# Diff heads' p, their rows and all of y turned by VectorE and transfers instead of TensorE, in a fused decoder layer

## The chip, the cores and the metric

The kernel runs on one core of a Trainium2 chip. Its engines each execute their own instruction stream in order: TensorE (PE, with PEld for the weight loads that overlap the matmuls), VectorE (DVE), ScalarE (ACT), GpSimd (POOL) and SyncE (SP). Here GpSimd issues transfers (its software queue) and SyncE issues the weight loads. The metric is the device time of one execution in microseconds (us).

## The reference

One decoder layer over 256 tokens of width 2048, in float32: a half-step SwiGLU feed-forward (5632 wide), layer norm, a token mixer with two attention branches, a projection and layer norm, a second feed-forward and a last layer norm. The branch that the change touches is differential attention, four heads of two score maps each:

```python
s = jnp.einsum('bqhmd,bkhmd->bhmqk', q[:, q0:q1], k[:, :q1]).astype(jnp.float32) * scale
...
p = jax.nn.softmax(s, axis=-1)
a = (p[:, :, 0] - lam * p[:, :, 1]).astype(v.dtype)
outs.append(jnp.einsum('bhqk,bkhd->bqhd', a, v[:, :q1]))
...
o_diff = (_rms_norm(o_diff, subln_g) * (1.0 - lambda_init)).reshape(b, s, DIFF_V_COLS)

y = jax.nn.sigmoid(gate_mla) * (o_mla @ w_br_mla) + jax.nn.sigmoid(gate_diff) * (o_diff @ w_br_diff)
return y @ w_out
```

The other branch is multi-head latent attention (MLA, eight heads), whose queries, keys and values come out of low-rank rows by `w_uq`, `w_uk` and `w_uv`. Queries are taken in blocks of 128, and the first block sees only the first 128 keys, so a head's probabilities are three 128x128 squares: a tile of 128x384.

## The kernel before

**Products.** Every large product is made of float32 parts rounded to the matmul's type: a value is split in a high part (a cast on ScalarE, line 154) and a low part (a subtraction on VectorE, line 155), and three matmuls (high by high, high by low, low by high: lines 208, 209, 210) make one product of a 128x128 stationary tile with 512 weight columns. Weights arrive raw by SP's queue and are split into a ring of six slots (`wring`). A unit of the program is the twelve matmuls of one weight tile of 128x1024 (two 128-row halves, two blocks of 128 tokens, three products each).

**Order.** The program is written in one stream. `unit()` and `advance()` keep a few units loaded and split ahead of the products, each unit ends with a `tick()`, and `later(n, fn)` puts work off by n ticks: transposes, softmax steps and copies are woven between the units by such numbers. A scheduler then fixes the order on each engine and places the semaphores; `issue_after` and `behind_split` tie one instruction behind another. Tiles called `blocks`, `turned`, `qr`, `junk`, `orow` and the like come from one pool of six slots (`tmp`), so a new one waits until the last reader of an old one, which may be a transfer, has ended.

**Stages.** First feed-forward (0 to 685 us): its hidden rows are turned by `turn_out` (VectorE transposes 32x32 blocks, line 715, and four GpSimd transfers write them to DRAM so that the rest of the turn is made by addresses, line 717), to be read back as `hraw` (line 893) and split as `h`. Layer norm and the mixer (685 to 1180), the output projection with a layer norm (1180 to 1320), and the second feed-forward (1320 to 1971), built as the first.

**The mixer's narrow part** (about 985 to 1180 us) runs `gate(1, 2)`, `wuq` (three column chunks), `wuk` (two), `wuv` (two), `gate(1, 3)`, `wbd` (four) and `wbm` (four). The four differential heads are woven between `gate(1, 2)` and `wuv`: `scores` (line 1228, then softmax), `turn` (three transposes of p by TensorE, line 1103, and a copy out of PSUM, line 1105), `values` (lines 1248 to 1250, then root mean square and `orow`, line 1261), and `turn2` (four transposes of `orow` by TensorE, line 1268, split straight into `od`, the left operand of `wbd`). They start six ticks apart. The MLA heads follow in the same manner and keep their transposes. `cols_proj` copies a projection's bank by ScalarE to a row tile (line 1160), turns it by `turn_out`, and reads it back by `turned` (line 729) for `qT` and `kT`; the rotary part `qr` goes the same way. In the output projection's left operand y, quads 0 and 1 are turned by transfers and quads 2 and 3 by TensorE (`rows_to_quad`, line 671).

Of the kernel before, what the change touches and what calls it, by code (L numbers as in the profile page):

```python
# [59 lines left out]
def layer_kernel(ctx: ExitStack, tc: tile.TileContext, a: dict, out: bass.AP):  # L60
# [89 lines left out]

    cast, lows, fetched = [None], [None], [None]

# [559 lines left out]
    def turn_out(row, to):  # L712

        t = tmp_tile([P, 512], "blocks")
        V.transpose(t, row)  # L715
        for i in range(4):
            nc.gpsimd.dma_start(to.rearrange("(g r) (i f) -> i r g f", g=4, i=4)[i],  # L717
                                t[32 * i:32 * (i + 1), :].rearrange("r (g f) -> r g f", g=4))
# [3 lines left out]

    def turn(row, use, wait, more):
        to = dram.tile([P, 512], F32, name=nm("turn"))
        turn_out(row, to)

        def back():
            t = tmp_tile([P, 512], "turned")
            nc.gpsimd.dma_start(t, to)
            later(more, lambda: use(turned(t)))  # L730
        later(wait, back)

    def turn_to_quad(row, b, x, q, wait, more):
        turn(row, lambda t: x.put(q, b, t), wait, more)

# [116 lines left out]
    def ffn(n, x, wgu, wdn, residual, g, bt, each, first=None, between=None, nxt=None, cols=None, norm=None, pending=None):  # L852
# [7 lines left out]
        def half(c, b, up, gate, wait=0):  # L860
# [7 lines left out]
            def product():  # L868
                V.tensor_tensor(out=hb[b, q][:, o:o + 256], in0=up, in1=sg, op=ALU.mult)
            if wait:  # L870
# [19 lines left out]
        def get_h(q):  # L890
            raw = got[q] = act_tile([P, 2, 512], F32, "hraw")
            for b in range(2):
                nc.gpsimd.dma_start(raw[:, b, :], hT[q, b])

# [205 lines left out]
    def p_cols(p):  # L1100
# [5 lines left out]
        return pt  # L1106

    def mixer(x):
        c_row = [act_tile([P, 1024], F32, "c_row") for _ in range(2)]
# [44 lines left out]

        def cols_proj(w, xx, kt, name, k0=0, more=10):
# [29 lines left out]
        def pair_cols(w, name):  # L1185
            dst = [act_tile([P, 4, T], F32, name) for _ in range(2)]

            def done(n, b, bank, snap, op):
                t = tmp_tile([P, 512], name + "r")
                whole(t, bank, snap, op)  # L1190
                later(1, lambda: turn_to_cols(t, dst[n], b, 4, 10))
            hy.group(w[0], w[1], done, False, True)
# [12 lines left out]
        def c_back(j):  # L1205
            if j == 0:
                for key, src in turns.items():
                    back[key] = tmp_tile([P, 512], "turned")
                    nc.gpsimd.dma_start(back[key], src)
# [6 lines left out]

        od = Acts(MH, "od")

        def diff_head(h):
# [21 lines left out]
            def turn():  # L1241
                st["pt"] = p_cols(st["p"])

            def values():
# [13 lines left out]
                r = rstd(ms, RMS_EPS, 2)  # L1258
                orow = tmp_tile([P, 512], "orow")
                for b in range(2):  # L1260
                    V.scalar_tensor_tensor(out=orow[:, b * DV:(b + 1) * DV], in0=o[:, b * DV:(b + 1) * DV],
                                           scalar=r[:, b:b + 1], in1=subg, op0=ALU.mult, op1=ALU.mult)
                st["o"] = orow

            def turn2():
                t = tr_bank()
                for i in range(4):
                    PE.transpose(t[:, i * P:(i + 1) * P], st["o"][:, i * P:(i + 1) * P], ident)
                tv = t.rearrange("p (b i t) -> p b i t", b=2, i=2)
                for b in range(2):  # L1270
                    od.put(h // 2, b, tv[:, b], (h % 2) * 2, 2)
            return scores, turn, values, turn2
# [8 lines left out]
        def qr_done(b, bank):  # L1281
            t = tmp_tile([P, 512], "qr")
            tv = t.rearrange("p (j h i) -> p j h i", j=2, h=MH)
            rope(tv[:, 0], tv[:, 1], bank, b, MH)
            later(1, lambda: turn_to_cols(t, qrT, b, 4, 10))
        project(a["wuq"][2], cn, 4, 512, qr_done)
        kT = [cols_proj(a["wuk"][c], cn, 4, "kT", 4, 8) for c in range(2)]
        v = [act_tile([P, 1024], F32, "v") for _ in range(2)]
# [56 lines left out]
        def branch_mla(f):  # L1345
# [87 lines left out]
def _layout(i):  # L1433
# [27 lines left out]
    r["wbm"] = _chunks(w["w_branch_mla"], 512)  # L1461
    r["wbd"] = _chunks(w["w_branch_diff"], 512)
    r["w_out"] = _chunks(np.concatenate([_turned_rows(w["w_out"][:1024]), w["w_out"][1024:]]), 512)
    pos = i["positions"]
# [32 lines left out]
```

## Time and profile before

| | |
|---|---|
| median of 3 runs | 1973.18 us (1972.44 to 1976.2) |
| the profiled execution | 1972.85 us, span 1971.1 us |
| TensorE busy | 1955.1 us (99% of the span), mean granted clock 0.998 |
| VectorE, ScalarE, GpSimd busy | 1773.5 us (90%), 1265.5 us (64%), 291.0 us (15%) |
| GpSimd's turn writes (`turn<-blocks`) | 104 of 64 KB, 3.4 us from issue to landing |

All times below are in us from the start of the span. A group's row gives the engine, the operation, the tiles out<-in, the count, then busy time and mean ns of one, then the idle time of the engine just before. A row of waits gives who waited for whom: us in total, times, and the longest. A row of the timeline gives start, duration, engine, line and operation. Matmuls overlap their successors, so the time from one start to the next is what a matmul takes of TensorE, not its own duration.

### The profile page before, as it was taken

Reading aid. Unit: us, or ns where it says so; the run is one execution under the profiler, and the core shown is the slowest. Engines: PE = TensorE matmul, PEld = TensorE weight load, DVE = VectorE, ACT = ScalarE, POOL = GpSimd, SP = SyncE. Lnnn points to the kernel's source line nnn. Section 1 sums busy time; section 2 is a strip of 40 time slices with the busy share of each in tenths; the row PEclk is TensorE's granted clock in tenths of the full one; section 3 lists DMA queues with packets and bytes.
Section 4 is the critical chain, followed back from the end, with each engine's and each line's share of the span. In section 5 each row is a group of like instructions: output and inputs, shape, how many; then the busy total and the mean of one; then the engine's idle time right before and its main releaser. Section 6 shows DMA issues by size and latency. Waiting matters only on the chain.

```text
span 1971.1 us, 25747 instructions
## 1 busy us (share of the span) xinstructions
PE 1955.1 (99%) x8784; PEld 1620.0 (82%) x8784; DVE 1773.5 (90%) x2175; ACT 1265.5 (64%) x1650; POOL 291.0 (15%) x503
## 2 busy tenths in 40 slices
PE   9999999999999999999999999999999999999997
PEld 7888888888888898888888888888888888888886
DVE  7999999999998879988976677789999999999986
ACT  6666767676655566666667765556676776665661
POOL 0112111122100010102223120001211112210000
PEclk9999999999999999999999999999999999999999
DMA  8978888777776666767667668578888878786763
GB/s 309 287 227 262 285 270 251 235 216 281 296 235 222 209 218 254 244 224 259 223 198 241 234 216 271 199 263 254 254 263 294 243 243 249 238 321 237 274 234 124
DMA packets 147478, 485.71 MB, mean 246 GB/s; under 512 B 20961, under 2 KB 21009, under 8 KB 147345
## 3 DMA queue, kind: packets, MB, share of 16 engines
q1 hardware_dynamic: 117360, 397.99, 58.2%
q0 software_dynamic: 29984, 86.07, 16.4%
q8 instruction: 69, 1.13, 0.2%
q14 instruction: 65, 0.52, 0.1%
HBM read 455.13 MB, written 28.84 MB: 246 GB/s over the span
## 4 chain that ended last, share of the span: by engine, by line
PE 95%; DVE 2%; DMA 1%; issue 1%; ACT 0%; SPq 0%; DVEq 0%; ACTq 0%
PE mm L209 30%; PE mm L210 30%; PE mm L208 30%; DVE wring L155 1%; PE tr L208 1%; PE tr L210 1%; PE tr L209 1%; DMA sraw<-in_gu_dram 1%; PE tr L671 0%; DVE sraw L428 0%; ACT wring L154 0%; DMA raw<-in_gu_dram 0%; PE tr L1228 0%; PE tr L1301 0%; PE tr L1303 0%
## 5 line engine op out<-in xcount | busy, mean ns | idle before, releaser
L154 ACT CAST wring<-raw 128x1024 fp32r<-128x1024 f32 (+2 forms) x467 | 482.2, 1038 | 296.5 <-PE mm L210 207.2
L155 DVE TENSOR_TENSOR wring<-raw,wring 128x1024 fp32r<-128x1024 f32 (+2 forms) x467 | 559.1, 1206 | 95.4 <-ACT wring L154 92.8
L154 ACT CAST wring<-sraw 128x1024 fp32r<-128x1024 f32 x436 | 454.8, 1054 | 230.2 <-DVE sraw L428 94.2
L155 DVE TENSOR_TENSOR wring<-sraw,wring 128x1024 fp32r<-128x1024 f32 x436 | 523.2, 1228 | 21.6 <-ACT wring L154 18.8
L210 PE MATMUL mm<-wring,h 128*128 128x512 f32 (+2 forms) x1248 | 480.2, 385 | 0.0
L208 PE MATMUL mm<-wring,h 128*128 128x512 f32 (+2 forms) x1248 | 480.2, 385 | 0.0
L209 PE MATMUL mm<-wring,h 128*128 128x512 f32 (+2 forms) x1248 | 479.8, 385 | 0.0
L209 PE MATMUL mm<-wring,xs 128*128 128x512 f32 x776 | 302.2, 389 | 1.3 <-DVE wring L155 1.3
L208 PE MATMUL mm<-wring,xs 128*128 128x512 f32 x776 | 302.2, 389 | 0.0
L210 PE MATMUL mm<-wring,xs 128*128 128x512 f32 x776 | 302.0, 389 | 0.0
L209 PEld LDWEIGHTS mm<-wring,h 128*128 128x128 f32 x1248 | 234.5, 188 | 46.8 <-DVE wring L155 0.7
L210 PEld LDWEIGHTS mm<-wring,h 128*128 128x128 f32 x1248 | 234.5, 188 | 46.5 <-DVE h L155 0.7
L208 PEld LDWEIGHTS mm<-wring,h 128*128 128x128 f32 x1248 | 234.4, 188 | 46.4 <-ACT h L154 0.6
L428 DVE TENSOR_TENSOR sraw<-sraw,sraw 128x1024 f32<-128x1024 f32 x168 | 200.2, 1229 | 3.5 <-DMA sraw<-in_wdv_dram 1.6
L209 PEld LDWEIGHTS mm<-wring,xs 128*128 128x128 f32 x776 | 145.7, 188 | 32.5 <-DVE wring L155 2.3
L208 PEld LDWEIGHTS mm<-wring,xs 128*128 128x128 f32 x776 | 145.7, 188 | 30.1
L210 PEld LDWEIGHTS mm<-wring,xs 128*128 128x128 f32 x776 | 145.7, 188 | 30.0
L717 POOL DMA_DIRECT2D hT<-blocks x176 | 97.1, 562 | 370.0 <-DVE blocks L715 368.2
L208 PE MATMUL mm<-wring,x 128*128 128x512 f32 x336 | 130.8, 390 | 0.8 <-ACT wring L154 0.8
L209 PE MATMUL mm<-wring,x 128*128 128x512 f32 x336 | 131.0, 390 | 0.5 <-DVE wring L155 0.5
L210 PE MATMUL mm<-wring,x 128*128 128x512 f32 x336 | 130.6, 389 | 0.0
L430 POOL DMA_DIRECT2D sraw<-in_gu_dram x40 | 35.6, 900 | 359.4 <-DVE sraw L428 309.0
(307 smaller groups left out, 2289.6 us busy)
## 6 DMA issues: line engine op xcount, KB each, us to landing
sraw<-in_gu_dram SPq DMA_DIRECT2D x160, 512.0 KB, 5.4
raw<-in_gu_dram SPq DMA_DIRECT2D x159, 512.0 KB, 4.7
raw<-in_dn_dram SPq DMA_DIRECT2D x140, 512.0 KB, 4.7
sraw<-in_gu_dram POOLq DMA_DIRECT2D x40, 512.0 KB, 6.9
sraw<-in_dn_dram SPq DMA_DIRECT2D x36, 512.0 KB, 5.6
hraw<-hT POOLq DMA_DIRECT2D x68, 256.0 KB, 6.2
eraw<-in_gu_dram SPq DMA_DIRECT2D x64, 256.0 KB, 6.0
raw<-in_w_out_dram SPq DMA_DIRECT2D x32, 512.0 KB, 4.3
```

Of the source, the lines that this page charges most:

```text
L154: cast[0] = S.copy(hi, src)
L155: lows[0] = V.tensor_tensor(out=lo, in0=src, in1=hi.bitcast(F32), op=ALU.subtract)
L208: PE.matmul(o, xh, wh, start=first, stop=False, skip_group_check=again)
L209: PE.matmul(o, xh, wl, start=False, stop=False, skip_group_check=again)
L210: PE.matmul(o, xl, wh, start=False, stop=last, skip_group_check=again)
L428: last = V.tensor_tensor(out=R[src][i], in0=R[src][i], in1=R[add[1]][i], op=ALU.add)
L430: nc.gpsimd.dma_start(R["12"][s], source("22", s), accum_op=ALU.add)
L717: nc.gpsimd.dma_start(to.rearrange("(g r) (i f) -> i r g f", g=4, i=4)[i], t[32 * i:32 * (i + 1), :].rearrange("r (g f) -> r g f", g=4))
```

## The change

It has five parts.

1. **p of the differential heads.** `p_cols` (three TensorE transposes, one ScalarE copy) gives way to `turn_p`: VectorE transposes p's 32x32 blocks into `pblocks` (128x384), one GpSimd transfer writes it to DRAM (`pturn`), and two ticks later four GpSimd transfers of 32 partitions each read it back in runs of 32 numbers (`pt<-pturn`).
2. **The heads' rows.** `turn2` goes. Two heads share an `orow` tile (from the larger pool of activation tiles), and after the second of a pair `turn_to_quad` turns both blocks: two VectorE transposes, eight transfers out, two back, and whole splits in place of half ones. `w_branch_diff` and `w_out` get their rows permuted on the host to match.
3. **All of y** goes through `turn_to_quad`, quads 2 and 3 with shorter waits.
4. **The projections' rows.** `cols_proj` hands the PSUM bank itself to the VectorE transpose (eight ScalarE copies go), with `more` 5 in place of 10 or 8; quads turned back get a tile of the larger pool (`roomy`).
5. **Places.** Heads start 5 ticks apart with steps at 0, 3 and 8; in the feed-forwards `get_h` is tied behind the last hidden write before it (`turned_out`), and the delayed `product` is tied behind a split.

```diff
+        with tc.issue_after(turned_out[0].ins):
+            for b in range(2):
+                nc.gpsimd.dma_start(raw[:, b, :], hT[q, b])
...
+    def turn_p(p, keep, more):
+        t = tmp_tile([P, 384], "pblocks")
+        V.transpose(t, p)
+        to = dram.tile([P, 384], F32, name=nm("pturn"))
+        nc.gpsimd.dma_start(to, t)
+        def back():
+            pt = small.tile([P, 384], F32, tag="p", name=nm("pt"), bufs=3)
+            for k in range(4):
+                nc.gpsimd.dma_start(pt[32 * k:32 * (k + 1), :].rearrange("f (b i c) -> f b i c", b=3, i=4),
+                                    to.rearrange("(i f) (b k c) -> k f b i c", i=4, b=3, k=4)[k])
+            keep["pt"] = pt
+        later(more, back)
...
             def done(b, bank):
-                t = tmp_tile([P, 512], name + "r")
-                S.copy(t, bank)
-                later(1, lambda: turn_to_cols(t, dst, b, 4, more))
+                later(1, lambda: turn_to_cols(bank, dst, b, 4, more))
...
             def turn():
-                st["pt"] = p_cols(st["p"])
+                turn_p(st["p"], st, 2)
...
-            def turn2():
-                t = tr_bank()
-                for i in range(4):
-                    PE.transpose(t[:, i * P:(i + 1) * P], st["o"][:, i * P:(i + 1) * P], ident)
-                tv = t.rearrange("p (b i t) -> p b i t", b=2, i=2)
-                for b in range(2):
-                    od.put(h // 2, b, tv[:, b], (h % 2) * 2, 2)
+                if h % 2 == 1:
+                    rows = orows.pop(h // 2)
+                    for b in range(2):
+                        later(2 + b, lambda b=b: turn_to_quad(rows[:, b, :], b, od, h // 2, 2, 3))
...
-                later(2 + 6 * h + 3 * i + i // 3, f)
+                later(1 + 5 * h + (0, 3, 8)[i], f)
...
-                if f < 2:
-                    later(1, lambda: turn_to_quad(y[:, b, :], b, yq, f, 4, 6))
-                else:
-                    later(2, lambda: rows_to_quad(y[:, b, :], b, yq, f))
+                later(1, lambda: turn_to_quad(y[:, b, :], b, yq, f, *((4, 6) if f < 2 else (3, 3) if f == 2 else (1, 2))))
```

**Head 2.** In the rows below the numbers behind a name tell tiles apart; heads are counted from 0. On GpSimd, before, the turns of `qr` and the first `kT` rows stand alone between one another:

```order
L717 DMA turn_8221<-blocks_8222 32x4x128 x4
L729 DMA turned_8253<-turn_8057 128x512
L717 DMA turn_8255<-blocks_8256 32x4x128 x4
L729 DMA turned_8281<-turn_8096 128x512
L717 DMA turn_8283<-blocks_8284 32x4x128 x4
L729 DMA turned_8316<-turn_8123 128x512
```

In the change the write of head 2's p (`pturn_8203`) and its reading back (`pt_8312`) have the two `qr` turns and the turn of the first pair's row (`turn_8305`, out of `blocks_8306`) between them:

```order
L1115 DMA pturn_8203<-pblocks_8201 128x384
L729 DMA turned_8205<-turn_8027 128x512
L717 DMA turn_8207<-blocks_8208 32x4x128 x4
L729 DMA turned_8239<-turn_8095 128x512
L717 DMA turn_8241<-blocks_8242 32x4x128 x4
L729 DMA turned_8303<-turn_8119 128x512
L717 DMA turn_8305<-blocks_8306 32x4x128 x4
L1120 DMA pt_8312<-pturn_8203 32x12x32 x4
L717 DMA turn_8317<-blocks_8318 32x4x128 x4
```

On VectorE, before, head 1's row (`orow_8178`) is followed by the softmax of the next head's scores and by two weight splits:

```order
L1261 SCALAR_TENSOR_TENSOR orow_8178<-tr_8154,f_8176,subg 128x256 x2
L1084 SCALAR_TENSOR_TENSOR st_8184<-tr_8181,bias_93 128x384
L1084 SCALAR_TENSOR_TENSOR st_8200<-tr_8197,bias_93 128x384
L1086 TENSOR_REDUCE mx_8186<-st_8184 128x1
L1087 TENSOR_REDUCE mx_8186<-st_8184 128x1
L715 STREAM_TRANSPOSE blocks_8222<-qr_8140 128x512
L1089 TENSOR_SCALAR nmx_8189<-mx_8186 128x2
L155 TENSOR_TENSOR wring_103<-raw_8392,wring_102 128x1024
L1071 TENSOR_TENSOR ropec_8247<-mm_8147,sincos 128x512
L155 TENSOR_TENSOR wring_5086<-raw_8477,wring_5085 128x1024
```

In the change the row of head 1 (`orow_8003`, shared with head 0) is followed by head 3's softmax, two weight splits, and then the transpose that `turn_8305` writes out:

```order
L1280 SCALAR_TENSOR_TENSOR orow_8003<-tr_8175,f_8197,subg 128x256 x2
L1086 SCALAR_TENSOR_TENSOR st_8268<-tr_8265,bias_94 128x384
L1086 SCALAR_TENSOR_TENSOR st_8284<-tr_8281,bias_94 128x384
L1088 TENSOR_REDUCE mx_8270<-st_8268 128x1
L1089 TENSOR_REDUCE mx_8270<-st_8268 128x1
L155 TENSOR_TENSOR wring_117<-raw_8524,wring_116 128x1024
L1091 TENSOR_SCALAR nmx_8273<-mx_8270 128x2
L155 TENSOR_TENSOR wring_115<-raw_8545,wring_114 128x1024
L715 STREAM_TRANSPOSE blocks_8306<-orow_8003 128x512
```

So GpSimd's reading of head 2's p now stands behind a transpose of head 1's finished row. On TensorE, the transposes of head 2's p and head 1's row before:

```order
L210 MATMUL mm_8337<-wring_114,cn_7861 128x512
L1103 MATMUL tr_8310<-ident,p_8191 128x128
L1268 MATMUL tr_8344<-ident,orow_8178 128x128 x2
L1103 MATMUL tr_8310<-ident,p_8191 128x128 x2
L1268 MATMUL tr_8344<-ident,orow_8178 128x128 x2
L208 MATMUL mm_8368<-wring_102,cn_7834 128x512
```

and around the values of head 2 in the change, which take `pt_8312`:

```order
L209 MATMUL mm_8459<-wring_103,cn_7856 128x512
L210 MATMUL mm_8459<-wring_102,cn_7857 128x512
L1265 MATMUL tr_8405<-dv_7343,pt_8312 128x256
L1266 MATMUL tr_8405<-dv_7343,pt_8312 128x256
L1267 MATMUL tr_8405<-dv_7344,pt_8312 128x256
L208 MATMUL mm_8473<-wring_5085,cn_7836 128x512
L209 MATMUL mm_8473<-wring_5086,cn_7836 128x512
```

What moved is the release of the values: from a ScalarE copy behind TensorE's own transposes to the last of four transfers on GpSimd's queue. From the values of head 0 to those of heads 1, 2 and 3 there are 79, 47 and 69 matmuls of 512 columns in the change (and head 3's scores just behind head 1's values).

**Head 3.** On VectorE, before, between the last `kT` transposes and head 2's `oms` (the first step of its root mean square) stand four weight splits:

```order
L715 STREAM_TRANSPOSE blocks_8356<-kTr_8335 128x512
L155 TENSOR_TENSOR wring_103<-raw_8587,wring_102 128x1024
L155 TENSOR_TENSOR wring_5086<-raw_8631,wring_5085 128x1024
L155 TENSOR_TENSOR wring_119<-raw_8648,wring_118 128x1024
L715 STREAM_TRANSPOSE blocks_8386<-kTr_8381 128x512
L155 TENSOR_TENSOR wring_117<-raw_8666,wring_116 128x1024
L1257 TENSOR_SCALAR oms_8418<-oss_8414 128x2
L690 TENSOR_SCALAR ve_8420<-oms_8418 128x2
```

In the change three transposes, each into a `blocks` tile of the pool of six, stand ahead of two splits, `oms` and the transpose of head 3's p:

```order
L715 STREAM_TRANSPOSE blocks_8345<-orow_8003 128x512
L715 STREAM_TRANSPOSE blocks_8352<-mm_8258 128x512
L715 STREAM_TRANSPOSE blocks_8380<-mm_8329 128x512
L155 TENSOR_TENSOR wring_5086<-raw_8630,wring_5085 128x1024
L155 TENSOR_TENSOR wring_119<-raw_8654,wring_118 128x1024
L1274 TENSOR_SCALAR oms_8413<-oss_8409 128x2
L1113 STREAM_TRANSPOSE pblocks_8432<-p_8275 128x384
```

and on GpSimd the write of head 3's p and the four reads come after the writes of those transposes, the reads divided by the turn of another `kT` row:

```order
L717 DMA turn_8351<-blocks_8352 32x4x128 x4
L729 DMA turned_8375<-turn_8207 128x512
L729 DMA turned_8377<-turn_8305 128x512
L717 DMA turn_8379<-blocks_8380 32x4x128 x4
L1115 DMA pturn_8434<-pblocks_8432 128x384
L729 DMA turned_8439<-turn_8344 128x512
L729 DMA turned_8437<-turn_8241 128x512
L1120 DMA pt_8494<-pturn_8434 32x12x32
L717 DMA turn_8441<-blocks_8442 32x4x128 x4
L729 DMA turned_8467<-turn_8317 128x512
L729 DMA turned_8488<-turn_8351 128x512
L1120 DMA pt_8494<-pturn_8434 32x12x32 x3
```

What moved here is that head 2's row of work and head 3's p on VectorE stand behind three turns, and that eight transfers of other tiles stand between the write of head 3's p and the last of its reads.

**The hidden rows.** In the first feed-forward four of GpSimd's rows stood behind an early hidden write, ahead of the weight loads of the next group:

```order
 L717 DMA hT_122<-blocks_1833 32x4x128 x4
 L717 DMA hT_122<-blocks_1839 32x4x128 x4
-L893 DMA hraw_3231<-hT_122 128x512
-L893 DMA hraw_3282<-hT_122 128x512 x2
-L893 DMA hraw_3231<-hT_122 128x512
```

In the change the first three quads (two transfers each) stand together behind the last but one group's hidden write:

```order
 L717 DMA hT_122<-blocks_3061 32x4x128 x4
 L717 DMA hT_122<-blocks_3067 32x4x128 x4
+L895 DMA hraw_3201<-hT_122 128x512 x2
+L895 DMA hraw_3231<-hT_122 128x512 x2
+L895 DMA hraw_3282<-hT_122 128x512 x2
 L430 DMA sraw_462<-in_gu_dram 128x1024
 L430 DMA sraw_463<-in_gu_dram 128x1024
```

The second feed-forward has the same shift. ScalarE's casts of the first of these quads go with them.

More of the change, by code (lines that the diff above doesn't have):

```diff
@@ L721, in turned, with turn @@
         return v.rearrange("p (i k c) -> p k i c", i=4, k=4)
-    def turn(row, use, wait, more):
+    def turn(row, use, wait, more, roomy=False):
         to = dram.tile([P, 512], F32, name=nm("turn"))
@@ L727, in back @@
         def back():
-            t = tmp_tile([P, 512], "turned")
+            t = act_tile([P, 512], F32, "turned") if roomy else tmp_tile([P, 512], "turned")
             nc.gpsimd.dma_start(t, to)
@@ L733, in turn_to_quad @@
     def turn_to_quad(row, b, x, q, wait, more):
-        turn(row, lambda t: x.put(q, b, t), wait, more)
+        turn(row, lambda t: x.put(q, b, t), wait, more, True)
     def turn_to_cols(row, dst, b, wait, more):
@@ L868, in product @@
             def product():
-                V.tensor_tensor(out=hb[b, q][:, o:o + 256], in0=up, in1=sg, op=ALU.mult)
+                with behind_split(3) if wait else nullcontext():
+                    V.tensor_tensor(out=hb[b, q][:, o:o + 256], in0=up, in1=sg, op=ALU.mult)
             if wait:
@@ L1206, in c_back @@
             if j == 0:
-                for key, src in turns.items():
-                    back[key] = tmp_tile([P, 512], "turned")
-                    nc.gpsimd.dma_start(back[key], src)
+                pairs = [act_tile([P, 2, 512], F32, "turned") for _ in range(2)]
+                for (i, b), src in turns.items():
+                    back[i, b] = pairs[i][:, b, :]
+                    nc.gpsimd.dma_start(back[i, b], src)
             if j >= 4:
```

28 lines of the change are left out of this document (14 added, 14 removed).

## The prediction

> **What bounds the kernel now.** First the page: the share of each engine, the granted clock, and the chain that ended last.
>
> ```profile
> span 1971.1 us, 25747 instructions
> PE 1955.1 (99%) x8784; PEld 1620.0 (82%) x8784; DVE 1773.5 (90%) x2175; ACT 1265.5 (64%) x1650; POOL 291.0 (15%) x503
> PEclk9999999999999999999999999999999999999999
> PE 95%; DVE 2%; DMA 1%; issue 1%; ACT 0%; SPq 0%; DVEq 0%; ACTq 0%
> ```
>
> TensorE is the bound: 16.0 us of the span are not busy, and 95% of the chain is its own. What it saves counts in full, and every wait of it counts too. Then the busy time by stretch: the narrow part of the mixer, and the two places where the early hidden rows are read back.
>
> ```profile
> 1006.00:1082.00 76.00, 74.69 (x346) 61.70 (x345) 56.08 (x123) 55.67 (x105) 28.43 (x52) 1.00 0.72 236
> 232.00:260.00 28.00, 27.27 (x121) 22.28 (x120) 26.06 (x32) 18.58 (x25) 7.85 (x13) 1.00 0.94 309
> 1498.00:1535.00 37.00, 36.47 (x161) 29.80 (x160) 35.38 (x42) 24.67 (x34) 9.22 (x15) 1.00 0.85 273
> ```
>
> In 1006 to 1082, where the differential heads lie, TensorE idles 1.3 us of 76, VectorE is 74% busy, and GpSimd issues 52 transfers. So the heads cost TensorE almost only their instructions. Last the timeline of TensorE, for what an instruction takes of it (start to start).
>
> ```profile
> 1025.71 0.39 PE L208 MATMUL mm<-wring,cn 128*128 128x512 f32 x1
> 1026.39 0.60 PE L1248 MATMUL tr<-dv,pt 128*128 128x256 f32 x2
> 1027.69 1.47 PE L1228 MATMUL tr<-dkT,dqT 128*128 128x128 f32 x8
> 1028.81 0.58 PE L208 MATMUL mm<-wring,cn 128*128 128x512 f32 x1
> 1042.61 0.27 PE L1103 MATMUL tr<-ident,p 128*128 128x128 f32 x1
> 1043.15 0.38 PE L1268 MATMUL tr<-ident,orow 128*128 128x128 f32 x2
> ```
>
> A triple takes 1026.39 - 1025.71 = 0.68, so a matmul of 512 columns 0.227; a head's values 1.30, its scores 1.12. Five transposes start between 1042.61 and 1043.15: 0.108 each.
>
> **What goes.** The groups and waits of the removed work:
>
> ```profile
> L1103 PE MATMUL tr<-ident,p 128*128 128x128 f32 x36 | 7.3, 284 | 0.2 <-DVE p L1237 0.2
> L1268 PE MATMUL tr<-ident,orow 128*128 128x128 f32 x16 | 3.1, 274 | 0.0
> L671 PE MATMUL tr<-ident,diff 128*128 128x128 f32 x16 | 2.4, 272 | 0.0
> L1248 PE MATMUL tr<-dv,pt 128*128 128x256 f32 x8 | 2.5, 392 | 1.1 <-ACT pt L1105 1.1
> ```
>
> Of the 36 transposes of p, 24 belong to the eight MLA heads and stay; 12 go, with 16 of `orow` and 16 of y. 44 x 0.108 = 4.8 us of TensorE. The wait of 1.1 for `pt` and the 0.2 for p go with them: 1.3. ScalarE's copies and half splits lie beside TensorE's matmuls (64% busy): nothing.
>
> The early reading of hidden rows, in the timeline of GpSimd:
>
> ```profile
> 237.20 2.17 POOL L893 DMA_DIRECT2D hraw<-hT  x4 [2.13 <-DMA hT<-blocks]
> 253.52 0.89 POOL L430 DMA_DIRECT2D sraw<-in_gu_dram  x1 [14.14 <-DVE sraw L428]
> 293.38 0.91 POOL L430 DMA_DIRECT2D sraw<-in_gu_dram  x1 [16.32 <-DVE sraw L428]
> ```
>
> The four reads end at 239.4, 14 us ahead of GpSimd's next weight load, so they don't hold the queue; what is lost at 232 to 260 (0.73 by the stretch) and at 1498 to 1535 (0.53) comes with their traffic or ScalarE's casts. The change puts six such reads behind a later hidden write, where no edge weights follow. The loss goes (1.3 gained), or moves along and grows by half (0.6 lost, 6 reads for 4). I take 0.8: the new place has less weight traffic. Gains: 4.8 + 1.3 + 0.8 = 6.9 us.
>
> **What comes.** Rows of the new work and of what it waits for:
>
> ```profile
> L717 POOL DMA_DIRECT2D turn<-blocks x104 | 56.8, 554 | 168.3 <-DVE blocks L715 139.8 <-DVE ms L1126 18.4 <-DVE nmx L1089 6.7
> turn<-blocks POOLq DMA_DIRECT2D x104, 64.0 KB, 3.4
> turned<-turn POOLq DMA_DIRECT2D x26, 256.0 KB, 4.3
> cols<-in_ln_cols_dram POOLq DMA_DIRECT2D x2, 16.0 KB, 3.5
> L715 DVE STREAM_TRANSPOSE blocks<-kTr 128x512 f32<-128x512 f32 x4 | 2.8, 707 | 5.2 <-DMA turn<-blocks 5.1
> DVE blocks L715 <- DMA turn<-blocks: 5.1, 1, 5.1
> ACT wring L154 <- PE mm L210: 269.9, 267, 5.9
> ```
>
> A turn write of four transfers is 2.2 us of GpSimd and lands 3.4 later; a transpose is 0.7 of VectorE; and a transpose has already stood 5.1 us for a turn write, the tile of the pool of six that it needed still being read. The four reads of p have no row: 384 runs of 128 bytes each. I take 0.55 for the issue, as every turn transfer, and 3.5 for the landing, that of `cols` (128 runs of 128 bytes). Three times the runs at three times the price (1.65) is the upper end; they can't be cheaper, being transfers from the same queue.
>
> *Head 2.* Count from the end of head 1's values. Before, that end is 1027.69, and the row follows so:
>
> ```profile
> 1027.89 0.39 ACT L1254 ACTIVATE junk<-tr 128x256 f32<-128x256 f32 x1 [0.25 <-PE tr L1250]
> 1029.74 0.17 DVE L1257 TENSOR_SCALAR oms<-oss 128x2 f32<-128x2 f32 x1
> 1031.18 0.88 DVE L1261 SCALAR_TENSOR_TENSOR orow<-tr,f,subg 128x256 f32<-128x256 f32 x2
> 1031.97 1.01 DVE L1084 SCALAR_TENSOR_TENSOR st<-tr,bias 128x384 f32<-128x384 f32 x2
> 1033.42 0.70 DVE L715 STREAM_TRANSPOSE blocks<-qr 128x512 f32<-128x512 f32 x1
> 1034.08 1.22 DVE L155 TENSOR_TENSOR wring<-raw,wring 128x1024 fp32r<-128x1024 f32 x1
> 1035.21 0.69 DVE L1071 TENSOR_TENSOR ropec<-mm,sincos 128x512 f32<-128x512 f32 x1
> ```
>
> `orow` is done 4.4 behind the values; st and the two mx take 1.4 (1031.97 to 1033.42). In the change two splits (start to start 1.13 each) and `blocks_8306` (0.7) follow: 4.4 + 1.4 + 2.3 + 0.7 = 8.8. Then `turn_8305` 2.2, the four reads 2.2, landing 3.5: 16.7. TensorE meanwhile has head 3's scores and 47 matmuls: 1.12 + 47 x 0.227 = 11.8. It waits 4.9 at least. In the change the rotary rows (transpose, ropec, ropes, two products, a split, a transpose) also stand between `oms` and `orow`: 3.0 more, and `blocks_8306` follows the landing of the second `qr` turn when it needs that tile: 0.8 more, so 20.5 and a wait of 8.7. I take 8.7, since each of those rows stands in the order; with reads at 1.65 it is 13.
>
> *Head 3.* Count from the start of head 2's values, the landing of `pt_8312`; GpSimd had issued it 3.5 before. `turn_8317` (2.2, landing 3.4) frees a tile for `blocks_8352` (0.7); `turn_8351` (2.2 + 3.4) one for `blocks_8380` (0.7); `turn_8379` (2.2 + 3.4) one for the squares of head 2: -3.5 + 5.6 + 0.7 + 5.6 + 0.7 + 5.6 = 14.7. Squares to `oms` as before 1029.74 - 1027.69 = 2.0, `pblocks` 0.6, `pturn` 0.55 and, between the landings of 64 KB and 256 KB, 3.8: 21.7. Then one read, `turn_8441`, two `turned` and three reads: 0.55 + 2.2 + 1.1 + 1.65 = 5.5, landing 3.5: 30.7. TensorE has 1.30 + 69 x 0.227 = 17.0. The wait is 13.7 if each transpose needs the tile of the write just before; if none does, the splits of `wring_5086` and `wring_119`, which need 12 matmuls behind the values and a cast (1.3 + 2.7 + 1.0), lead to `oms` at 6.5 and the last read at 20.4: 3.4. I take 11, nearer to the end that the row of 5.1 us shows at work.
>
> *The rest.* Head 0's p stands ahead of the `qr` turns, and 79 matmuls (17.9 us) lie between its values and head 1's: its reads and head 1's are nothing, or 1.5 where head 1's follow the first `qr` writes. `od`'s second pair: `orow` 4.4, transposes 1.4, eight writes 4.4, landing 3.4, back 0.55 + 4.3, splits 1.3: 19.8 behind head 3's values, against the 69 matmuls of `wuv`, the gate and `od`'s first pair (15.7) and MLA head 0's scores (1.3): 0 to 2.8, and I take 1, as nothing else stands on GpSimd's queue by then. y's last quad: 0.7 + 2.2 + 3.4 + 0.55 + 4.3 + 1.3 = 12.5, with six units of `w_out` (12 x 0.227 each, 16.3) ahead of its use: nothing, up to 3 if quad 2's transfers come between. `cols_proj` reading its bank by VectorE costs a transpose either way.
>
> Sum: -6.9 + 8.7 + 11 + 1 = +13.8 on the profiled execution's 1972.85: 1986.6; the median lies 0.3 above that execution: 1987. Own range: 1974 (waits of 4.9 and 3.4, nothing else) to 1994 (8.7, 13.7, 2.8 and 3).
>
> The clock: the trace starts from rest, and there 24 passes of 128 columns took 5.69 - 1.06 = 4.63 us, 0.193 each, where later ones take 0.108.
>
> ```profile
> 1.06 4.88 PE L98 MATMUL tr<-zero 128*128 128x128 f32 x24 [1.06 <-DVE zero L96]
> 5.69 0.48 PE L208 MATMUL mm<-wring,x 128*128 128x512 f32 x1
> ```
>
> So a restart may cost 4.63 - 24 x 0.108 = 2.0 us. The page's clock reads 9 in every slice; of the waits shown none exceeds 1.1 us. Behind head 2's wait this is mostly taken from head 3's, whose chain is not TensorE's; it stays within the range. [...]
>
> **The rivals.**
>
> - *Transfers hidden, faster.* The reads of p land in time. For it: GpSimd is 15% busy, and before the narrow part lost 1.3 us with 52 transfers. Against it: 16.7 against 11.8 at the loosest count. It decides at 4.9 us: if `blocks_8306` is done 3.9 us behind head 1's values and not 8.8, nothing waits. Then -6.9: 1966, with 1963 to 1970.
> - *Only head 2 waits.* The chain of tiles doesn't bind and head 3 is 3.4 or less: 4.9 to 8.7 + 0 to 3.4 - 6.9, 1971 to 1978, likeliest 1975.
> - *Small runs are dear.* Each read takes 1.65: 4.4 more on GpSimd per head, in heads 2 and 3, and 1 to 3 in head 1: 1996, with 1993 to 2003. [...]
>
> **How the numbers follow.** The forecast of two waits 0.52, transfers hidden 0.24, only head 2 0.13, dear runs 0.11. Below 0.2% (3.9 us, about what a measurement of this kernel can tell from no change) are the times from 1969 to 1977: two thirds of the third case and a little of the others: same 0.10. Faster: the second, and a little of the third: 0.26. Slower: 0.64. The range from 1966 to 1997 leaves out half of the hidden case and two thirds of the dear one: 0.19.
>
> **What would show it.** The waits of the changed kernel: TensorE's values behind a transfer `pt<-pturn`, twice, 9 and 11 us (right); a row below 2 us (hidden). GpSimd's `turn` behind VectorE's `blocks` and VectorE's `blocks` behind `turn` transfers, longer than 5.1. The issue of `pt` at 0.55 or 1.65, its landing at 3.5. The granted clock in the slices about 1050 and 1075. No idle at 253 and 1527, and none at 413 and 1688 either. The forecast is wrong if the stretch 1006 to 1082 of before keeps its 1.3 us of idle.

## The result and the profile after

The changed kernel takes 1999.28 us (median of 4 runs, 1999.01 to 2003.21) against 1973.01 before: ratio 1.0134, 95% interval 1.0117 to 1.0152, 26 us slower. It was forecast slower, but by 14 us, and the time lies above both ranges of the forecast (1974 to 1994, and the wider 1966 to 1997).

The page of the changed kernel, with the lines that answer to those shown of before:

```profile
span 1996.6 us, 25745 instructions
PE 1961.1 (98%) x8740; PEld 1622.1 (81%) x8740; DVE 1779.1 (89%) x2183; ACT 1254.2 (63%) x1632; POOL 324.7 (16%) x563
...
PEclk9999999999999999999998999999999999999999
...
PE 90%; DMA 4%; DVE 3%; issue 2%; ACT 1%; POOL 1%; SPq 0%; DVEq 0%; POOLq 0%; ACTq 0%
```

TensorE issues 44 instructions less and is busy 6.0 us longer, over a span 25.5 us longer. One slice of its clock shows 8 where all were 9, and the chain now goes by transfers, VectorE and waits for a tenth of the span. By stretches (busy time of PE, PEld, DVE, ACT, POOL, then the granted clock):

```profile
1006.00:1085.00 79.00, 65.68 (x262) 52.40 (x261) 51.14 (x110) 42.22 (x76) 43.62 (x77) 0.89 0.73 222
1048.00:1054.00 6.00, 5.49 (x12) 3.80 (x12) 3.06 (x9) 2.30 (x6) 5.18 (x10) 0.51 0.51 151
1072.60:1078.00 5.40, 5.35 (x13) 4.23 (x14) 2.71 (x5) 4.67 (x9) 2.73 (x5) 0.52 0.61 193
1185.00:1260.00 75.00, 68.84 (x289) 55.35 (x287) 53.15 (x65) 33.68 (x40) 16.86 (x31) 0.95 0.80 268
1225.50:1231.00 5.50, 5.41 (x13) 4.21 (x14) 1.92 (x2) 1.08 (x2) 0.56 (x1) 0.50 1.02 373
```

and the output projection before, where TensorE has no gap:

```profile
1185.00:1230.00 45.00, 45.00 (x204) 37.24 (x203) 33.20 (x39) 22.23 (x26) 0.00 (x0) 1.00 0.82 267
```

Two stretches lose: the differential heads (TensorE idle 13.3 us of 79, where it was 1.3 of 76) and the output projection (6.2 of 75). In both, matmuls run for some microseconds behind a wait at a granted clock of about half (0.50 to 0.52 in the rows above). Along the program, the first product of `wbm` comes 16.5 us later than before, the first transpose of the second layer norm 24.6, the end 25.5.

The waits of the heads' part, and what stood where (the timeline's columns are start, duration, engine, line and operation, and the wait just before):

```profile
PE mm L208 <- ACT v L1304: 4.4, 1, 4.4
PE mm L208 <- DVE blocks L715: 4.2, 2, 2.4
PE mm L208 <- DVE nmx L1091: 3.5, 1, 3.5
PE tr L1265 <- DMA pt<-pturn: 1.2, 1, 1.2
DVE blocks L715 <- DMA turn<-blocks: 5.7, 3, 4.2
```

```profile
1035.28 1.47 PE L1245 MATMUL tr<-dkT,dqT 128*128 128x128 f32 x8
1046.21 0.71 DVE L715 STREAM_TRANSPOSE blocks<-orow 128x512 f32<-128x512 f32 x1 [0.24 <-DMA turn<-blocks]
1047.39 0.71 DVE L715 STREAM_TRANSPOSE blocks<-mm 128x512 f32<-128x512 f32 x1
1048.16 0.79 PE L208 MATMUL mm<-wring,cn 128*128 128x512 f32 x1 [3.47 <-DVE nmx L1091]
1048.75 0.63 PE L209 MATMUL mm<-wring,cn 128*128 128x512 f32 x1
1049.18 0.63 PE L210 MATMUL mm<-wring,cn 128*128 128x512 f32 x1
1050.20 2.68 POOL L1120 DMA_DIRECT2D pt<-pturn  x4
1054.86 0.70 PE L1265 MATMUL tr<-dv,pt 128*128 128x256 f32 x2 [1.22 <-DMA pt<-pturn]
1058.82 0.47 PE L208 MATMUL mm<-wring,cn 128*128 128x512 f32 x1 [2.40 <-DVE blocks L715]
1062.84 0.72 DVE L715 STREAM_TRANSPOSE blocks<-mm 128x512 f32<-128x512 f32 x1 [4.16 <-DMA turn<-blocks]
1063.61 0.50 PE L208 MATMUL mm<-wring,cn 128*128 128x512 f32 x1 [1.81 <-DVE blocks L715]
1069.26 0.38 ACT L1271 ACTIVATE junk<-tr 128x256 f32<-128x256 f32 x1
```

Head 1's values end at 1035.28, where the scores of head 3 begin. The transpose of the finished row (`blocks<-orow`, 1046.21), which GpSimd's reads of head 2's p follow, ended 11.6 us behind them. But TensorE stopped earlier, for a bank of PSUM (a tile `mm`, which the matmuls write): the next transpose reads `wuk`'s bank (1047.39, to 1048.10), and only its end lets the matmul at 1048.16 start. (The row names `nmx`, a small step of the softmax that VectorE ended just then; the matmul doesn't read it. The wait is gone where the banks are copied first, below.) `wuk`'s next two banks hold TensorE in the same way at 1058.82 and 1063.61. Behind the wait at 1048.16 one matmul takes 0.43 of TensorE (1048.75 to 1049.18), not 0.227. The reads of p are issued from 1050.20, landing at 1054.8, and the values wait only 1.2 for them, since TensorE had already stood still. The squares of head 2 (1069.26) wait for the chain of turn writes, as recorded, and what TensorE then waits for is not head 3's p but the copy of v behind the squares on ScalarE, which holds a bank: 4.4. From the chain that ended last (start, duration, what):

```profile
1053.22 0.44 PE mm L210
1053.73 1.05 ACT wring L154
1055.94 0.71 DVE blocks L715
1066.55 1.96 DMA turn<-blocks
```

The last write lands at 1068.51 and frees the tile that the squares need. The chain itself begins behind TensorE: the matmul at 1053.22 frees a slot of `wring`, ScalarE casts into it, VectorE splits it, and only then comes the row's second transpose (1055.94), with which the writes up to the squares begin.

What a transfer cost, by the groups and issues:

```profile
L1120 POOL DMA_DIRECT2D pt<-pturn x16 | 10.8, 746 | 3.0 <-DMA pturn<-pblocks 3.0
pt<-pturn POOLq DMA_DIRECT2D x16, 48.0 KB, 3.7
```

The output projection, on GpSimd, VectorE and TensorE:

```profile
1206.85 0.71 DVE L715 STREAM_TRANSPOSE blocks<-diff 128x512 f32<-128x512 f32 x1
1208.78 0.55 POOL L717 DMA_DIRECT2D turn<-blocks  x1
1212.35 0.56 POOL L729 DMA_DIRECT2D turned<-turn  x1 [3.02 <-DMA turn<-blocks]
1212.90 3.25 POOL L717 DMA_DIRECT2D turn<-blocks  x6
1219.07 0.56 POOL L729 DMA_DIRECT2D turned<-turn  x1 [2.92 <-issue]
1219.84 0.40 PE L210 MATMUL mm<-wring,y 128*128 128x512 f32 x1
1225.57 0.69 DVE L155 TENSOR_TENSOR y<-turned,y 128x512 fp32r<-128x512 f32 x1 [6.58 <-ACT y L154]
1225.59 0.80 PE L208 MATMUL mm<-wring,y 128*128 128x512 f32 x1 [5.36 <-ACT y L154]
```

A quad is 512 columns of y, in two blocks of 128 tokens. Quad 3's first block is transposed at 1206.85; one of its four writes goes at 1208.78, and the other three stand behind the reading back of quad 2 (1212.35), which waits 3.0 for a landing. From transpose to split it is 18.7 us. TensorE had matmuls until 1220.2, 13.4 us from that transpose, and then waited 5.4. The second block's last write stands behind the first block's reading back (1219.07), and from there the chain that ended last goes by transfers (a write, then the reading back):

```profile
1219.62 6.25 DMA turn<-blocks
1226.44 6.35 DMA turned<-turn
```

At 1233.48, behind a wait of 0.8, TensorE takes that block.

### The profile page after: what moved, and what is told of

It is laid out like the page before. It is cut to its first block, busy times and chain, and to the rows that moved or that the text cites. A ratio compares the mean times of both kernels' runs of the same rounds, so it can differ in the third digit from the quotient of the medians.

```text
span 1996.6 us, 25745 instructions
## 1 busy us (share of the span) xinstructions
PE 1961.1 (98%) x8740; PEld 1622.1 (81%) x8740; DVE 1779.1 (89%) x2183; ACT 1254.2 (63%) x1632; POOL 324.7 (16%) x563
## 4 chain that ended last, share of the span: by engine, by line
PE 90%; DMA 4%; DVE 3%; issue 2%; ACT 1%; POOL 1%; SPq 0%; DVEq 0%; POOLq 0%; ACTq 0%
PE mm L209 29%; PE mm L208 29%; PE mm L210 29%; DMA turn<-blocks 2%; DVE wring L155 1%; DMA sraw<-in_gu_dram 1%; PE tr L208 1%; PE tr L210 1%; PE tr L209 1%; DMA turned<-turn 1%; POOL turn L717 1%; PE tr L671 0%; DVE sraw L428 0%; DVE blocks L715 0%; ACT wring L154 0%
## 5 line engine op out<-in xcount | busy, mean ns | idle before, releaser
L717 POOL DMA_DIRECT2D turn<-blocks x136 | 74.7, 561 | 176.5 <-DVE blocks L715 149.2
```

The lines of the kernel that those rows point to most:

```text
L717: turned_out[0] = nc.gpsimd.dma_start(to.rearrange("(g r) (i f) -> i r g f", g=4, i=4)[i], t[32 * i:32 * (i + 1), :].rearrange("r (g f) -> ...
```

## The experiments

All kernels start from the changed kernel; "put back" is a part as it was before. Times are medians, ratios are against the kernel before on the same chip. Its medians there lie between 1972.4 and 1973.8, so a difference of about 1 us between two runs tells nothing.

**One part put back at a time.** y's last quads by TensorE (the rows of `w_out` go back with them):

```diff
-later(1, lambda: turn_to_quad(y[:, b, :], b, yq, f, *((4, 6) if f < 2 else (3, 3) if f == 2 else (1, 2))))
+if f < 2: later(1, lambda: turn_to_quad(y[:, b, :], b, yq, f, 4, 6))
+else: later(2, lambda: rows_to_quad(y[:, b, :], b, yq, f))
```

> The changed kernel with y's quads 2 and 3 turned by TensorE again (and w_out's rows for them as before); all else as in the change. Theory (y's last quads come too late for the output projection, 6.5 us of waits and 2.7 us of matmuls at half rate behind them): the waits between 1215 and 1240 go, 16 transposes (1.7) come back, so about 8 us less than the changed kernel, 1991. Rival (the wait there is for weights or for the layer norm's loads): within 2 us of the changed kernel's 1999.

1992.16, ratio 1.0097 (1.0082 to 1.0112): 7.1 less. TensorE is busy for all of 1185 to 1260:

```profile
1185.00:1260.00 75.00, 75.00 (x340) 62.13 (x339) 58.23 (x69) 38.17 (x45) 6.60 (x12) 1.00 0.81 267
```

So y's last quads cost 7.1, near the 8 of the theory.

The hidden rows' reads untied:

```diff
-with tc.issue_after(turned_out[0].ins):
-    for b in range(2):
-        nc.gpsimd.dma_start(raw[:, b, :], hT[q, b])
+for b in range(2):
+    nc.gpsimd.dma_start(raw[:, b, :], hT[q, b])
```

> The changed kernel without the tie of the hidden rows' reads behind the last hidden write. Theory (six reads behind one write are dearer than two and four: the two stalls grew from 1.0 and 0.8 to 2.2 and 1.6): the stalls go back to their old places and sizes, 1.8 us less, 1997.5. Rival (the stalls come from the product's tie behind a split, which stays): no change, 1999.

1996.96, ratio 1.0125 (1.0108 to 1.0142), 2.3 less. The intervals overlap, so the size by these times is uncertain, but TensorE's waits for weight splits behind the later reads (1.7 us between 400 and 425 and 1.2 between 1700 and 1725 in the changed kernel's waits) are gone, and one of 0.5 stands in the second feed-forward, between 1540 and 1560. The other traces bear it out. From the first transpose of the second layer norm to the end, the eight kernels here that keep the tie take 0.6 to 1.2 us longer than the kernel before, and the eleven without it from 0.8 less to 0.2 more.

p by TensorE and ScalarE:

```diff
-turn_p(st["p"], st, 2)
+st["pt"] = p_cols(st["p"])
```

> The changed kernel with the differential heads' p turned by TensorE and copied by ScalarE as before; spacing, rows, y and the rest as in the change. Theory (TensorE waits in the heads' part for PSUM banks whose transposes stand behind turn writes on a pool of six tiles; p's 20 transfers lengthen that queue but are not alone): part of the 19 us of waits and half-rate matmuls there goes, 1988 to 1995. Rival (p's transfers alone are the cause): all of it goes but 12 transposes come back, 1982. Rival (p does not matter, banks do): 1998 or more.

1996.29, ratio 1.012 (1.0105 to 1.0135): 3.0 less, with intervals that overlap, and a smaller gain than either the theory or the first rival said. The waits for banks stay, 5.5 for transposes and 4.4 for v.

The eight banks copied by ScalarE first:

```diff
+t = act_tile([P, 512], F32, name + "r")
+S.copy(t, bank)
-later(1, lambda: turn_to_cols(bank, dst, b, 4, more))
+later(1, lambda: turn_to_cols(t, dst, b, 4, more))
```

> The changed kernel with the eight query and key banks copied by ScalarE to a row tile (of the large pool) before VectorE turns them, so that a bank is free after the copy. Theory (waits for the banks hide a wait for p behind them, by the recorded count 8.7 and 11 us): the waits named by banks go, waits of the values for the reads of p take their place, 1992 to 1999. Rival (the banks are the cause by themselves): the heads' part loses nothing, 1981 to 1984.

1998.8, ratio 1.0133 (1.0118 to 1.0148): 0.5 less, nothing that can be told. The waits of the heads' part are:

```profile
PE tr L1267 <- DMA pt<-pturn: 7.7, 1, 7.7
PE mm L208 <- ACT v L1306: 4.5, 1, 4.5
```

Freed of the banks, TensorE waits 7.7 for head 2's p. The two waits hide each other, and the recorded count for head 2 (8.7) was near in size.

**Several put back.** p and the bank copies together:

> The changed kernel with p turned by TensorE and with ScalarE's copies of the query and key banks, both at once; the heads' rows and y still by transfers. Theory (two causes in a row, banks and reads of p, each hiding the other: one alone gave 3 and 0.5): together more than the sum, 1985 to 1991, what is left in the heads' part being the wait for v behind the squares. Rival (the parts add): 1996.

1987.16, ratio 1.0071 (1.0056 to 1.0086): 12.1 less, where 3.0 and 0.5 make 3.5. What is left in the heads' part is mostly v's copy behind the squares, which wait for turn writes:

```profile
ACT junk L1273 <- DMA turn<-blocks: 8.7, 1, 8.7
PE mm L208 <- ACT v L1306: 3.6, 1, 3.6
```

The heads' rows alone by TensorE (turn2 and the rows of `w_branch_diff` as before, steps at 0, 3, 8 and 12):

```diff
-if h % 2 == 1:
-    rows = orows.pop(h // 2)
-    ...
+def turn2():
+    t = tr_bank()
+    for i in range(4): PE.transpose(t[:, i * P:(i + 1) * P], st["o"][:, i * P:(i + 1) * P], ident)
+    ...
```

> The changed kernel with the heads' rows turned by TensorE again (four transposes a head, split straight into the left operand); p, banks and y as in the change. Theory (the two transposes of the finished rows and their eight transfers stand ahead of p's reads in VectorE's and GpSimd's order): head 2's p is read earlier, the waits in the heads' part fall by half, 1988 to 1994. Rival (the kT turns and p's own route suffice to hold TensorE): 1997 to 2001.

1983.05, ratio 1.0049 (1.0034 to 1.0064): 16.2 less, more than the theory said, and the largest of the single parts.

The parts by themselves, each on a kernel with the others put back (the first has them all put back, with the new spacing left; its edits are those above together):

> The changed kernel with p, the heads' rows, y's last quads, the hidden reads and the bank copies all put back: what is left of the change is the spacing of five ticks, the earlier return of turned columns, the larger pool for turned quads and the product's tie. Theory (the loss lies in the parts put back): 1971 to 1975. Rival (the spacing itself crowds GpSimd's queue): 1980 or more.

1972.04, ratio 0.9994 (0.9985 to 1.0004): the loss lies in the parts put back, not in the spacing or in what else is left of the change.

> The heads' rows by transfers alone: the changed kernel with p, the bank copies, y's last quads and the hidden reads put back (the run that also put the rows back took 1972). Theory (the rows' turn is the largest single cause, by the squares of head 2 and v's copies that wait behind it): 1975 to 1979, with one wait of about 4 for v's copy and a half-rate stretch. Rival (the rows cost only together with p's reads): 1969 to 1972, 1.7 less than without them.

1976.14, ratio 1.0016 (1.0007 to 1.0025): rows alone cost 4.1. The wait is v's copy, 3.6.

> The changed kernel with the heads' rows, y's last quads and the hidden reads put back; p by transfers and banks read by VectorE stay. Theory (p's route is nearly harmless once no rows stand ahead of its reads): 1983 less 8 for y and 2 for the hidden reads, 1972 to 1976. Rival (p's own reads cost several us): 1977 or more.

1973.71, ratio 1.0007 (0.9998 to 1.0016): p and the bank reads alone cost 1.7, with intervals that overlap, so perhaps nothing.

> p, the heads' rows and the bank reads as in the change, y's last quads and the hidden reads put back. Theory (these parts hold each other up: rows alone cost 4.1, p and banks 1.7, together far more than 5.8): 1988 to 1992. Rival (they add): 1978.

1988.97, ratio 1.0082 (1.0067 to 1.0097): p, banks and rows together cost 17, about three times the 5.8 that they cost apart.

**The pool and the queue.** Eight small tiles for six (and 40 large ones for 41), on the changed kernel and on the last one:

```diff
-SLOTS = 41
+SLOTS = 40
-return small.tile(shape, dt, tag="tmp", name=nm(name), bufs=6)
+return small.tile(shape, dt, tag="tmp", name=nm(name), bufs=8)
```

> The changed kernel with eight tiles in the small pool instead of six (and 40 large activation tiles instead of 41); nothing else. Theory (VectorE's transposes and ScalarE's squares of head 2 wait for turn writes that still read a tile of the six): the waits named by turn writes shrink, TensorE's wait of 4.4 for ScalarE's copy of v and part of those for banks go, with a half-rate stretch of 2 behind each: 1988 to 1994. Rival (GpSimd's queue and the order alone hold p's reads and the banks): within 2 of 1999.

1991.01, ratio 1.0095 (1.008 to 1.011): 8.3 less.

> The same with eight tiles in the small pool instead of six. Theory (half of what the parts cost together is the wait for tiles that turn writes still read; the rest is p's reads behind the rows' writes on GpSimd, 7 to 8 us for head 2): 1981 to 1985. Rival (the pool is all of it): 1973 to 1976.

1981.48, ratio 1.004 (1.0027 to 1.0053): 7.5 less than with six. The waits left are

```profile
PE tr L1264 <- DMA pt<-pturn: 6.6, 1, 6.6
PE mm L208 <- DVE blocks L715: 3.1, 2, 1.7
PE mm L208 <- ACT od L154: 1.4, 2, 1.0
```

The wait for v is gone: it came through the pool, which is 7.5 of the 17. Head 2's p still comes 6.6 late. That the rest of the 17 is this wait, by GpSimd's queue, is read from the waits and was not tested by itself.

The first pair's rows turned eight ticks later, so that their writes come behind the reads of p on GpSimd:

```diff
-later(2 + b, lambda b=b: turn_to_quad(rows[:, b, :], b, od, h // 2, 2, 3))
+later((10 if h < 2 else 2) + b, lambda b=b: turn_to_quad(rows[:, b, :], b, od, h // 2, 2, 3))
```

> The changed kernel with the first pair's rows turned eight ticks later, so that on GpSimd their writes stand behind the reads of head 2's and head 3's p; the number of transfers and all else as in the change. Theory (place, not number: what stands ahead of p's reads holds them): the waits for banks, p and v in the heads' part fall by more than half, 1984 to 1991. Rival (the number of transfers on one queue and the pool of six): 1996 or more.

2006.59, ratio 1.0173 (1.0157 to 1.0189): slower than the change, so the theory of place alone falls. The waits move:

```profile
PE tr L1265 <- DMA pt<-pturn: 7.0, 2, 4.7
PE mm L208 <- ACT v L1304: 4.8, 1, 4.8
PE mm L208 <- ACT od L154: 4.0, 1, 4.0
```

Now heads 2 and 3 both wait for p, and the left operand of `wbd` comes late as well. This is one other place; whether there is a place for the rows' transfers in these 80 us that nobody waits behind was not tried further.

**y by itself and by its order.** All of y by transfers with the other four parts put back (the new spacing stays), and the same with other waits:

> All of y by transfers in the change's own order, with p, the heads' rows, the bank copies and the hidden reads put back (the same with y's last quads put back too took 1972.0). Theory (y's cost is its own and adds: 5 to 7 us of waits and half-rate matmuls, less 1.7 for the transposes): 1978 to 1981. Rival (it is large only behind the heads' delay): 1971 to 1974.

1978.42, ratio 1.0029 (1.0018 to 1.004): 6.4 over the run with all put back, much the 7.1 seen from the other side.

```diff
-(3, 3) if f == 2 else (1, 2)
+(4, 2) if f == 2 else (2, 1)
```

> As the run with all of y by transfers, but with quad 2's reading back four ticks behind its write (then two to the split) and quad 3's two ticks (then one), so that on GpSimd the four writes of quad 3's first block stand ahead of quad 2's last read. Theory (GpSimd's reads wait in the queue for the landing of writes, and the next writes stand behind them: 18.7 us from the transpose to the split where the transfers alone sum to 12.5): half of the loss or more goes, 1972 to 1976. Rival (the transfers' length alone, beside the loads of the layer norm): 1978 or more.

1972.88, ratio 0.9999 (0.999 to 1.0009): 5.5 of the 6.4 are gone. On GpSimd the four writes of quad 3's first block now go one behind the other, ahead of quad 2's last read, and the waits of the output projection fall from the first row to the second and third:

```profile
PE mm L208 <- ACT y L154: 4.6, 2, 4.0
```

```profile
POOL turned L729 <- DMA turn<-blocks: 7.8, 2, 4.0
PE mm L208 <- ACT y L154: 2.3, 1, 2.3
```

So it was mostly the order on the queue: the number of transfers is the same.

**A version that beats both.** Three were tried. The first has p, rows, banks and hidden reads put back, p's transposes two ticks later, and of y's last two quads only quad 2 by transfers; the others have the same but all of y in the better order and a last step at 13 ticks for 12, and the last of them eight small tiles. Against the steps above:

```diff
-later(1 + 5 * h + (0, 3, 8, 12)[i], f)
+later(1 + 5 * h + (0, 5, 8, 12)[i], f)
```

> A version meant to beat both: heads five ticks apart with p's transposes two ticks later (steps at 0, 5, 8 and 12), p and rows by TensorE, banks copied by ScalarE, hidden reads untied, and of y only quad 2 by transfers (quad 3, the last, by TensorE). Theory: eight transposes (0.9) and a wait of 1.8 for p less than the run with all put back (1972.0): 1969.5. Rival (quad 2's transfers stall the output projection): 1973 or more.

1972.12, ratio 0.9994 (0.9986 to 1.0003).

> A version meant to beat both: all of y by transfers in the better order, p, the heads' rows and the bank copies by TensorE and ScalarE, hidden reads untied, heads five ticks apart with steps at 0, 5, 8 and 13. Theory: the wait of 2.0 for p and one of 1.0 for a row go from the run with y in the better order (1972.9, span 1969.6): 1969.5 to 1971. Rival (nothing left to gain that a measurement can tell): 1972 to 1973.

1974.09, ratio 1.0 (0.9991 to 1.0009).

> The same with eight tiles in the small pool instead of six and one large tile fewer. Theory: transposes no longer wait for turn writes, 0 to 1 us less than with six. Rival (the missing large tile costs a wait elsewhere): 1 to 3 us more.

1974.04, ratio 0.9998 (0.9989 to 1.0006). None is faster than before by more than can be told: 8 or 16 transposes less (0.9 or 1.7 us) are within the spread of the runs, and TensorE still waits 3.1 for the last quad of y in the second of these. None reached the 1969.5 to 1971 that was expected. By the traces the heads' part (from the scores at 946 to the first product of `wbm`) is 2.4 and 2.8 us shorter than before in the last two, but the stretch behind it, with y, is 3.7 and 5.1 longer; their heads' part with y's last quads by TensorE was not tried.

## Why the prediction was right and wrong

- **The bound and the direction** held: TensorE is 95% of the chain before, so each wait counts, and the change adds waits on GpSimd's queue and the pool of six that outweigh the 44 transposes it saves.
- **The rivals.** Transfers hidden: no; the rows' transpose was done 11.6 us behind head 1's values, not 3.9. Only head 2 waits: no, there was a second wait behind the squares. Dear runs: no; a read of p took 0.75 of GpSimd and landed in 3.7, near the 0.55 and 3.5 that were taken and far from 1.65.
- **Head 2** (8.7) and **head 3** (11): the chains were the right ones, and the places where TensorE pays were not. It stood for `wuk`'s banks and for v's copy (3.5 + 4.2 + 4.4), and only 1.2 for p. The step that missed this is "`cols_proj` reading its bank by VectorE costs a transpose either way": it ties a bank to VectorE's order, where the transpose stands behind rows and turn writes. With the banks copied the wait for head 2's p is 7.7, close to 8.7; in the changed kernel the wait for the bank, the half rate behind it and the wait for p make 3.5 + 2.4 + 1.2 = 7.1 up to the same landing. Head 3's p was not waited for in the changed kernel; the squares that the count gave for 14.7 behind head 2's values (the start of the chain) came 14.4 behind them, 1054.86 to 1069.26, but v's copies stood behind these and held TensorE first. In all TensorE idled 13.3 us in the part where 20.7 of waits were forecast.
- **The clock** was held to stay within the range: a restart behind head 2's wait (2.0 by the estimate) "is mostly taken from head 3's, whose chain is not TensorE's". Here the step failed. There were four stretches of half rate, behind the waits of 3.5, 1.8, 4.4 and 5.4, with some 43 matmuls of 0.43 in all: 43 x 0.2 = 8.6 us, where none was in the sum. For two of them the step was right. The one behind 1.8 lies beside the turn writes that the squares wait for, and the one behind 5.4 ahead of the wait for quad 3's second block, which would else be longer. The other two, some 5 us, are not taken up. The first lies ahead of the wait for p, but it also moved the weight split that stands on VectorE ahead of the row's second transpose, so that the chain called head 3's did go by TensorE. Behind v's there is no wait near.
- **The heads' part as a whole** came out near by luck in part: 16.4 was forecast for it (8.7 + 11 + 1 - 1.3 - 3.0 for 28 transposes), and 15.6 came (16.5 at the first product of `wbm`, less 0.9 at its beginning). Waits of 13.3 where 20.7 were forecast, and some 6 us of half rate where none was, nearly cancel.
- **y's last quad** is the largest miss; without it the time would lie in the range. The step is "12.5, with six units of `w_out` (12 x 0.227 each, 16.3) ahead of its use: nothing, up to 3 if quad 2's transfers come between". They came between, and both terms were wrong. The way took 18.7 for 12.5: its four writes were issued in some 7 us for 2.2, as three of them stood behind the reading back of quad 2, and its own reading back took 5.9 from issue to cast (1219.07 to 1224.92) for 4.3. TensorE's work ahead of the use was 13.4 for 16.3. The difference is the wait of 5.4. The second block came later still, with its last write behind that reading back. The waits of 6.2, the half rate of some 2.6 between them and the 1.7 saved make the 7.1 us of loss.
- **The hidden rows**: 0.8 gained was forecast, the other end of that step (moves along and grows, 0.6 lost) was the case and larger, 2.3 lost by the run that unties them. The idle that was to be gone at 413 and 1688 is there, 1.5 at 418 and 1.0 at 1716. The new place was taken to have less weight traffic; why TensorE waits longer there was not shown.
- **The sum again.** y: 8.8 more than forecast (7.1 lost where 1.7 was counted as saved); hidden rows: 3.1 more (2.3 lost for 0.8 gained); the heads' part 0.8 less. 13.8 + 8.8 + 3.1 - 0.8 = 24.9, of the 26 measured. The 2.3 is the least certain of these terms.

## What to carry to other kernels

A transfer that replaces a few matmuls must be counted with the queue it joins: reads that wait for a landing stop the writes behind them, as the reading back at 1212.35, with its wait of 3.0, did with three of quad 3's writes. Parts that cost 4.1 and 1.7 us by themselves cost 17 together; that each took the slack that another lived on is the likely reason. When an engine takes over a read of PSUM, look at what stands ahead of it in that engine's order, since the bank, and the matmuls that need it, now wait for all of it (3.5, 2.4 and 1.8 us here). And where TensorE is the bound, look for matmuls at half rate behind a wait of a few microseconds (here some 2.5 us more behind each of the waits of 3.5, 4.4 and 5.4) and add them to it, unless the next wait is sure to take them up.

## What the runs showed of the hardware

Behind some waits the granted clock was about half in the changed kernel: 0.51, 0.52 and 0.50 in the stretches behind the waits of 3.5 at 1048, 4.4 at 1073 and 5.4 at 1226, with matmuls 0.43 apart for 0.227. The waits of 1.2 at 1054 and of 1.5 at 418 left no such stretch: from 1054 to 1058.8 and from 418 to 424 the clock was 1.00. The length of the wait alone doesn't decide it in this trace. Behind the wait of 2.4 at 1058.8 the matmuls run at full rate,

```profile
1058.00:1063.00 5.00, 2.98 (x12) 2.17 (x12) 0.84 (x2) 0.00 (x0) 3.96 (x9) 1.00 0.69 210
```

and behind the one of 1.8 at 1063.6, which comes soon after, they fall to 0.43 from 1064.18 to 1067.59. The four stretches at half rate last 5.3 us (from 1048.16), 3.4 (from 1064.18), 5.2 (from 1072.65) and 5.7 (from 1225.59). Behind the first comes the wait of 1.2; behind the other three the matmuls are 0.23 to 0.29 apart. What sets the length of such a stretch was not shown.
